# A hybrid decoder step on one core: the decode reads its cache tiles at a fixed place in the product stream, and the FFN norm's column sums move behind the first index's products

## The chip, the core and the metric

The kernel runs on one core of a Trainium2 chip. The time is the device time of one execution, in microseconds (us). The core has a matrix engine (PE, with its weight loads as PEld), a vector engine (DVE), a scalar engine (ACT), a general engine (POOL) and a queue engine (SP). Each works through its own list of instructions in order; semaphores tie them together, and DMA queues move data beside them. POOL issues the gathers of the decode cache, SP nearly all other loads.

## What is computed

One layer of a decoder, for a prompt of 512 tokens and for eight decode samples with a past of 2048 tokens each, in float32:

```python
a = rms_norm(x, attn_norm); proj = a @ w_in
# 8 stick-breaking attention heads (prompt: causal; sample: over the paged cache)
z = q.k * SCALE + bias;  log_1m_beta = log_sigmoid(z) - z
att = exp(log_sigmoid(z) + reverse_cumsum(log_1m_beta) - log_1m_beta);  o_sb = rms_norm(att @ v)
# 8 gated DeltaNet heads: conv width 4, silu, l2 norm, decay g, chunked recurrence on a state
s = s * exp(g) + k (beta * (v - k.s));  o_gdn = rms_norm(q.s) * silu(z_gate)
h = x + concat(o_sb, o_gdn) @ w_out
f = rms_norm(h, ffn_norm)
h = h + (silu(causal_dwconv(f @ w_gate)) * (f @ w_up)) @ w_down
h = h + (p @ w_ple_proj) * sigmoid(rms_norm(h, ple_norm) @ w_ple_gate);  y = rms_norm(h, final_norm)
```

For the samples, `k` and `v` of the attention are 2 x 64 MB of cache rows picked by a page table, and the DeltaNet state `s` is 4 MB.

## The kernel before

All 520 tokens (512 and 8) stand as two halves of 260 columns. A product is sixteen steps of the contraction in three float32r splits (high by high, high by low, low by high) in two halves: 96 matmuls, with the weights cut in `weights` (L234) into a high part (`wh`, ACT, L242) and a low part (`wl`, DVE, L243), one pair for each half-product of eight steps. The text counts places in the mixing stage by these half-products.

**Stages.** Up to about 85 us norm and a small projection; then 56 products with `w_in`; between them, on queues called lanes, the chains of each head (`sb_chain`, `k_chain`, `gdn_chain`, `invert`). A chain is a generator that yields the time after which it wants to go on; `tick` (L205) moves a clock by 0.65 for each step of a product and runs the chains that are due. Their small matmuls go through `mmq` and `trq` (L222, L226), which pin them behind the product matmul issued last. Then `w_out` in two parts: part 0 takes twelve of the sixteen heads (16 products of 72 matmuls), part 1 the last four heads (16 of 48). The half-products are counted from 1; `w_out` starts with number 113. From 1214 us on the FFN runs: 43 indices of `strassen` (seven block products each, names `pa` to `pd`), then `w_down`, the gate of the per-layer input and the last norm.

**Decode.** The cache comes as 128 tiles `kv` of 1 MB (32 of K for four heads, 32 of V, and the same for the other four), in two buffers. `gather` (L405) issues four indirect DMAs for each on POOL. Each K tile is used by four DVE instructions `dacc` (L435), each V tile by four `junk` (L465); after the last K tile stand a softplus, a scan and a small matmul `pc`. The DeltaNet state is read in four tiles (`rec`), with `gtmp` (L1013) and reduces (L1015) on DVE, in `delta_decode` (L965); its result `mix_s[2]` goes into the columns of the samples of heads 8 to 15, ahead of part 0 of `w_out`.

These calls stand in the program at a few points. What they issue has a priority far behind (`later(30000)`), so that the scheduler, which places each instruction by simulated time, puts them wherever an engine would else be idle:

```python
    with tc.issue_after(last.ins):
        decode_v(0, 0, AFTER)
    decode_v(0, AFTER)
```

Here the first two V tiles of the first four heads are pinned behind the last instruction of a triangular solve (`X`, L679 to L681). `AFTER` and `VSPLIT` are both 2: `decode_v(1, 0, 2)` stands ahead of `delta_decode()`, `decode_v(1, 2)` behind it.

**FFN norm.** While `w_out` part 1 ends, each row block `h` is squared on ACT (`sqt`) and summed by accumulating DMAs into two tiles `acc` (L1166). `rstd_of` (L278) sums these over partitions with matmuls (`ssq`, L286) and builds the scale `rb` (L288). It is called behind the first `strassen`, with matmuls that nothing pins.

## Time and profile before

| | us |
|---|---|
| median of 3 runs (lowest, highest) | 2807.46 (2803.03, 2808.61) |
| the profiled execution, its own time | 2818.48 |
| its span, first to last instruction | 2816.7 |
| PE busy | 2665.9 |
| DVE busy | 1900.4 |
| ACT busy | 1158.0 |
| POOL busy | 707.0 |

The rows below come from the profiled execution. A start is counted in us from the start of its span. `[3.60 <-DMA kv]` means: the engine stood idle for 3.60 us before this instruction, and a DMA into `kv` ended that. A busy PE is not PE at its peak; the granted clock (PEclk) says how fast it was allowed to run, 1.00 for 2.4 GHz, 0.50 for 1.2 GHz.

### The profile page before, as it was taken

The numbers are of one execution on the slowest core, as the hardware profiler recorded it, in microseconds if no ns is written. First come the engines' busy times: TensorE is split into PE (matmuls) and PEld (weight loads), VectorE is DVE, ScalarE is ACT, GpSimd is POOL, SyncE is SP. The second block draws the span as 40 slices with busy tenths as digits, with TensorE's granted clock in tenths as the row PEclk, the third lists the DMA queues.
The fourth block names the chain that finished last, engine by engine and source line by source line (L and its number), as shares of the span: only waits on it lengthen the run. The fifth ranks groups of instructions, "written<-read, shape, count | busy, mean of one in ns | idle before, by whom it ended". The sixth has DMA issues, their size and how long they took to land.

```text
span 2816.7 us, 52568 instructions
## 1 busy us (share of the span) xinstructions
PE 2665.9 (95%) x21329; PEld 2601.5 (92%) x21329; DVE 1900.4 (67%) x3060; ACT 1158.0 (41%) x1936; POOL 707.0 (25%) x773
## 2 busy tenths in 40 slices
PE   8998899899899988979999999999999999999997
PEld 7898788898898878979999999999998999999997
DVE  7477766667779776678888888888885242433545
ACT  5454434333345542554444444444452121322433
POOL 4565646556650556210000000000000000000000
PEclk9999999999999999989999999999999999999998
DMA  5778777767775778676555656565657453433333
GB/s 187 229 248 263 226 209 240 230 218 238 245 239 151 245 239 257 178 220 177 164 175 162 183 160 177 161 179 163 177 158 243 133 155 92 136 98 93 111 114 114
DMA packets 194083, 519.99 MB, mean 185 GB/s; under 512 B 41712, under 2 KB 51824, under 8 KB 193328
## 3 DMA queue, kind: packets, MB, share of 16 engines
q1 hardware_dynamic: 138672, 336.13, 37.3%
q0 software_dynamic: 55168, 180.50, 22.1%
q8 instruction: 167, 2.74, 0.4%
q14 instruction: 76, 0.62, 0.1%
HBM read 463.05 MB, written 49.76 MB: 182 GB/s over the span
## 4 chain that ended last, share of the span: by engine, by line
PE 59%; DVE 12%; DMA 11%; issue 9%; POOL 4%; ACT 3%; SPq 1%; another core or an unknown queue 0%; DVEq 0%; POOLq 0%; ACTq 0%
PE mm L264 27%; PE pb L1197 13%; PE pc L1197 9%; PE pa L1197 4%; POOL kv L408 4%; PE pd L1197 4%; DMA kv<-in_ck,idx 3%; DMA kv<-in_cv,idx 3%; DVE dacc L435 2%; DVE wl L243 2%; DMA acc<-sqt 2%; DVE junk L465 1%; DVE yg L610 1%; DVE dpart L1015 1%; DMA out_recs<-st 1%
## 5 line engine op out<-in xcount | busy, mean ns | idle before, releaser
L264 PE MATMUL mm<-ah,wl 128*128 128x260 f32 x4128 | 858.5, 289 | 27.3 <-DVE wl L243 21.9
L264 PE MATMUL mm<-ah,wh 128*128 128x260 f32 x4128 | 862.0, 290 | 14.1 <-ACT wh L242 11.0
L264 PE MATMUL mm<-al,wh 128*128 128x260 f32 x4128 | 855.3, 288 | 4.4 <-DVE al L373 3.1
L264 PEld LDWEIGHTS mm<-ah,wl 128*128 128x128 f32 x4128 | 651.2, 192 | 38.4 <-DVE wl L243 26.8
L264 PEld LDWEIGHTS mm<-ah,wh 128*128 128x128 f32 x4128 | 652.5, 192 | 22.2 <-ACT wh L242 12.6
L264 PEld LDWEIGHTS mm<-al,wh 128*128 128x128 f32 x4128 | 650.8, 192 | 8.8 <-DVE al L373 3.9
L242 ACT CAST wh<-w 128x1024 fp32r<-128x1024 f32 (+4 forms) x289 | 279.6, 968 | 670.9 <-PE mm L264 588.9
L243 DVE TENSOR_TENSOR wl<-w,wh 128x1024 fp32r<-128x1024 f32 (+4 forms) x282 | 315.7, 1120 | 232.2 <-ACT wh L242 218.9
L408 POOL DMA_INDIRECT kv<-in_cv,idx x256 | 282.2, 1102 | 275.7 <-DVE junk L465 86.5
L408 POOL DMA_INDIRECT kv<-in_ck,idx x256 | 287.3, 1122 | 188.2 <-DVE dacc L435 89.3
L1192 ACT CAST wh<-a 128x1024 fp32r<-128x1024 f32 x172 | 181.0, 1052 | 368.0 <-PE pc L1197 193.0
L465 DVE SCALAR_TENSOR_TENSOR junk<-kv,dacc 128x512 f32<-128x512 f32 x256 | 176.4, 689 | 104.2 <-DMA kv<-in_cv,idx 82.2
L1193 DVE TENSOR_TENSOR wl<-a,wh 128x1024 fp32r<-128x1024 f32 x172 | 210.0, 1221 | 46.2 <-ACT wh L1192 46.0
L435 DVE SCALAR_TENSOR_TENSOR dacc<-kv,qd,dacc 128x512 f32<-128x512 f32 x252 | 178.3, 746 | 90.9 <-DMA kv<-in_ck,idx 69.4
L1197 PE MATMUL pb<-ah,wl 128*128 128x260 f32 x774 | 221.5, 286 | 1.5 <-DVE wl L1193 1.3
L1197 PE MATMUL pb<-ah,wh 128*128 128x260 f32 x774 | 219.8, 284 | 0.6 <-ACT wh L1192 0.6
L1197 PE MATMUL pb<-al,wh 128*128 128x260 f32 x774 | 219.3, 283 | 0.0
L1356 POOL TENSOR_TENSOR y<-h,fr 128x260 f32<-128x260 f32 x8 | 6.9, 887 | 682.2 <-DVE fr L1351 682.2
L1197 PEld LDWEIGHTS pb<-ah,wl 128*128 128x128 f32 x774 | 147.0, 190 | 3.5 <-DVE wl L1193 2.7
L597 POOL MEMSET cbf<- 128x2 f32 x43 | 4.3, 99 | 573.4 <-DVE yf L610 566.4
L1197 PEld LDWEIGHTS pb<-ah,wh 128*128 128x128 f32 x774 | 146.5, 189 | 1.4 <-ACT wh L1192 1.4
L1197 PEld LDWEIGHTS pb<-al,wh 128*128 128x128 f32 x774 | 146.8, 190 | 0.0
(435 smaller groups left out, 4741.1 us busy)
## 6 DMA issues: line engine op xcount, KB each, us to landing
w<-in_w_in SPq DMA_DIRECT2D x112, 512.0 KB
a<-in_w_up SPq DMA_DIRECT2D x86, 512.0 KB
w<-in_w_down SPq DMA_DIRECT2D x48, 512.0 KB
w<-in_w_gate SPq DMA_DIRECT2D x43, 512.0 KB
s<-in_w_up SPq DMA_DIRECT2D x43, 512.0 KB
a<-in_w_gate SPq DMA_DIRECT2D x43, 512.0 KB
s<-in_w_up POOLq DMA_DIRECT2D x43, 512.0 KB
w<-in_w_pg SPq DMA_DIRECT2D x32, 512.0 KB
```

The lines of the kernel that those rows point to most:

```text
L242: S.copy(wh, w)
L243: last_wl[0] = (eng or V).tensor_tensor(wl, w, wh.bitcast(F32), op=ALU.subtract).ins
L264: last_mm[0] = PE.matmul(ps[:, hf, 0:HALF], lhsT=a, rhs=b[:, hf * HALF:(hf + 1) * HALF], start=(first and n == 0), stop=(last and n == 2)).ins
L408: G.indirect_dma_start(out=t[:, pg], out_offset=None, in_=src, in_offset=bass.IndirectOffsetOnAxis(ap=idx[:, g, dc, pg:pg + 1], axis=0))
L435: V.scalar_tensor_tensor(a2[dd % 2], kt[:, :, d], qd[:, dd:dd + 1], a2[dd % 2], op0=ALU.mult, op1=ALU.add)
L465: V.scalar_tensor_tensor(junk, vt[:, :, d], 1.0, A, op0=ALU.mult, op1=ALU.mult, accum_out=ov[:, dc * DC + d:dc * DC + d + 1])
L610: V.scalar_tensor_tensor(y, cb[:, j:j + L], cw[:, j:j + 1], y, op0=ALU.mult, op1=ALU.add)
L1015: V.tensor_reduce(part, tmp.rearrange("p k v -> p v k"), axis=AX.X, op=ALU.add)
L1192: S.copy(wh, w)
L1193: V.tensor_tensor(wl, w, wh.bitcast(F32), op=ALU.subtract)
L1197: last_mm[0] = PE.matmul(ps, lhsT=a[:, k], rhs=b, start=(start and k + n == 0), stop=(k == NP - 1 and n == 2), skip_group_check=not start).ins
L1356: e.tensor_tensor(y[:, j], hres[m + j][:, c], r, op=ALU.mult)
```

## The change

One generator, `decode()`, on a lane of its own called `kv`, takes the place of the three kinds of calls. It takes the tiles in one order: K and V of heads 0 to 3, K of heads 4 to 7, eleven V tiles (`DELTA`), the four state tiles of the DeltaNet, and the other 21 V tiles. It asks to be resumed every 4.1 of the clock (`PACE`). Each time it places the instructions of one tile behind the last `wl` issued (`paced`), with a priority of 60 instead of 30000, and then issues the loads of the next tile but one into the buffer it frees. There are still two buffers; the state tiles now pass through them as tiles like the others. The decode's small matmuls go through `mmq` and `trq`. The pin on the solve's last instruction stays only as the value that `last_dve` holds from there to the next `wl`.

Ahead of part 0 of `w_out` the program runs the lane until the DeltaNet's result is there, and ahead of part 1 until it is done. The memset of the 24 tiles `cbg` goes from POOL to DVE. `rstd_of` behind the first index takes `mmq`. Three small stores of the state's decode go into `delta_decode`, and in `w_down` the load of these and the start of the state's update move from index 1 to indices 2 and 4.

```diff
-LATE = 30000
-VSPLIT = 2
-AFTER = 2
+PACE = 4.1
+DELTA = 11
...
+        if eng is None:
+            last_dve[0] = last_wl[0]
...
-    def rstd_of(parts, rp):
+    def rstd_of(parts, rp, mm=None):
+        mm = mm or PE.matmul
...
-                PE.matmul(ps[:, 0:HALF], lhsT=ones, rhs=a[:, c], start=(n == 0), stop=(n == len(parts) - 1))
+                mm(ps[:, 0:HALF], ones, a[:, c], start=(n == 0), stop=(n == len(parts) - 1))
...
+    kv_items = [(n, g, dc) for g in range(2) for n in ("ck", "cv") for dc in range(NDC)]
+    at = 3 * NDC + DELTA
+    kv_items[at:at] = [("rec", 0, c) for c in range(4)]
...
+    def kv_fetch():
+        if not kv_items:
+            return
+        n, g, dc = kv_items.pop()
         t = dpool.tile([P, 4, DC * PAGE], F32, name="kv", bufs=2)
+        kv_ring.append((n, g, dc, t))
+        if n == "rec":
+            nc.sync.dma_start(t.rearrange("p a c -> p (a c)"), i["rec"][:, dc * 2048:dc * 2048 + 2048])
+            return
         for pg in range(4):
-            G.indirect_dma_start(out=t[:, pg], out_offset=None, in_=src,
+            G.indirect_dma_start(out=t[:, pg], out_offset=None, in_=i[n],
...
+    def paced():
+        st = contextlib.ExitStack()
+        if last_dve[0] is not None:
+            st.enter_context(tc.issue_after(last_dve[0]))
+        st.enter_context(later(60))
+        return st
...
+    def pace():
+        kv_time[0] += PACE
+        return max(0.0, kv_time[0] - clock[0])
...
+            for dc in range(NDC):
+                if g and dc == DELTA:
+                    while not cs_ready:
+                        yield 1.0
+                    yield from delta_decode()
+                yield pace()
+                vt = kv_take("cv", g, dc).rearrange("p g (d t) -> p g d t", d=DC)
+                with paced():
+                    for d in range(DC):
+                        junk = n4(dpool.tile([P, 8 * PAGE], F32, name="junk")[:, :4 * PAGE])
+                        V.scalar_tensor_tensor(junk, vt[:, :, d], 1.0, A, op0=ALU.mult, op1=ALU.mult,
+                                               accum_out=ov[:, dc * DC + d:dc * DC + d + 1])
+                kv_fetch()
...
-        G.memset(cb[:, 0:hw], 0.0)
+        (G if rs is not None else V).memset(cb[:, 0:hw], 0.0)
...
-    with tc.issue_after(last.ins):
-        decode_v(0, 0, AFTER)
-    decode_v(0, AFTER)
+    last_dve[0] = last.ins
...
         if part:
-            drain("sb")
+            drain("sb", "kv")
+        else:
+            until("kv", ("dec", 2))
...
-            rstd[0] = rstd_of(accs, npool)
+            rstd[0] = rstd_of(accs, npool, mmq)
...
-                    if m == 1:
+                    if m == 2:
...
-                if m == 1:
+                if m == 4:
                     spawn("upd", delta_update(*kvg, gpool))
```

What the built programs hold at three places follows, first of before, then of after. On DVE, where the solve of `X` ends and the first V tile is used (`tb` and `X` are the solve's):

```order
L681 TENSOR_TENSOR X<-X,tb 128x3x29
L679 TENSOR_TENSOR tb<-blk,X 128x60
L681 TENSOR_TENSOR X<-X,tb 128x2x30
L679 TENSOR_TENSOR tb<-blk,X 128x31
L681 TENSOR_TENSOR X<-X,tb 128x31
L465 SCALAR_TENSOR_TENSOR junk,ov<-kv,dacc_1199 128x512
L685 COPY XT<-X 128x1024
L465 SCALAR_TENSOR_TENSOR junk,ov<-kv,dacc_1199 128x512
```

```order
L722 TENSOR_TENSOR tb<-blk,X 128x112
L724 TENSOR_TENSOR X<-X,tb 128x4x28
L506 SCALAR_TENSOR_TENSOR junk,ov<-kv,dacc_1332 128x512
L722 TENSOR_TENSOR tb<-blk,X 128x87
L812 SCALAR_TENSOR_TENSOR osb<-osb,vec,sqh 128x512
L506 SCALAR_TENSOR_TENSOR junk,ov<-kv,dacc_1332 128x512
L724 TENSOR_TENSOR X<-X,tb 128x3x29
L842 SCALAR_TENSOR_TENSOR z<-pz,mb 128x128
L506 SCALAR_TENSOR_TENSOR junk,ov<-kv,dacc_1332 128x512
```

The first tile's four `junk` and two of the next now stand between the last steps of the solve, and no longer behind them.

On PE, the DeltaNet decode's two last small matmuls (`po<-cst,of`, then `pn`), which `mix_s[2]` waits for; `po<-z,vtok` belongs to an attention chain, `ah_11085` is head 8, the first of `w_out` part 0 whose sample columns come from `mix_s[2]`:

```order
L264 MATMUL mm<-al_504,wh 128x260 x2
L264 MATMUL mm<-ah_503,wl 128x260 x2
L264 MATMUL mm<-ah_505,wh 128x260
L1031 MATMUL po<-cst,of 128x64
L264 MATMUL mm<-ah_505,wh 128x260
L264 MATMUL mm<-al_506,wh 128x260 x2
```

```order
L222 MATMUL pi<-sm,ones 128x384
L222 MATMUL po<-z,vtok 128x512
L222 MATMUL po<-z,vtok 128x384
L222 MATMUL po<-z,vtok 128x256
L222 MATMUL po<-z,vtok 128x128
L222 MATMUL po<-cst,of 128x64
L222 MATMUL pn_9941<-sq_9891,ones 128x64
L265 MATMUL mm<-ah_11085,wh 128x260 x2
L265 MATMUL mm<-al_11086,wh 128x260 x2
```

Before, the first of them lay inside a product of `w_in`; now both lie inside the first half-product of `w_out`, right ahead of the matmul that needs the result, and behind the chain's.

On PE, where the FFN begins (`ssq` are the norm's column sums, `pb` and `pa` block products of the first index, `pc` its third):

```order
L264 MATMUL mm<-ah_12728,wh 128x260 x2
L264 MATMUL mm<-al_12729,wh 128x260 x2
L264 MATMUL mm<-ah_12728,wl 128x260 x2
L286 MATMUL ssq<-acc_13371,ones 128x260 x2
L286 MATMUL ssq<-acc_13372,ones 128x260 x2
L1197 MATMUL pb<-ah_13331,wh 128x260
L1197 MATMUL pb<-al_13332,wh 128x260
```

```order
L1237 MATMUL pc<-ah_13369,wh 128x260
L1237 MATMUL pc<-al_13370,wh 128x260
L1237 MATMUL pc<-ah_13369,wl 128x260
L222 MATMUL ssq<-acc_13371,ones 128x260 x2
L222 MATMUL ssq<-acc_13372,ones 128x260 x2
L1237 MATMUL pb<-al_13338,wh 128x260
```

The eight passes of `ssq` moved from ahead of the first block product to 190 rows behind it, past all the block products of the first index and into those of the second.

## Rows read from the trace of the kernel before

**Rows 1.** The page: engine, busy us (share of the span), instructions.

```profile
PE 2665.9 (95%) x21329; PEld 2601.5 (92%) x21329; DVE 1900.4 (67%) x3060; ACT 1158.0 (41%) x1936; POOL 707.0 (25%) x773
```

**Rows 2.** Busy time by stretch: from:to, length, engines, granted clock, DMA share, GB/s.

```profile
833.00:914.00 81.00, 77.78 (x609) 73.48 (x607) 74.32 (x136) 46.67 (x88) 5.08 (x4) 1.00 0.57 174
914.00:1140.00 226.00, 201.86 (x1442) 185.76 (x1443) 160.62 (x368) 90.51 (x136) 130.33 (x120) 0.95 0.75 244
1140.00:1214.00 74.00, 73.78 (x606) 72.72 (x604) 51.72 (x96) 48.62 (x89) 18.39 (x27) 1.00 0.69 188
1214.00:1242.00 28.00, 13.29 (x59) 11.14 (x60) 17.57 (x30) 12.69 (x23) 4.74 (x7) 0.63 0.83 237
```

**Rows 3.** What PE waited for, 60 to 1130 us: us, times, longest.

```profile
PE mm L264 <- DVE wl L243: 15.2, 12, 3.4
PE po L224 <- ACT z L835: 8.3, 3, 3.9
```

**Rows 4.** The cache tile kv: duration min/median/max in ns, first to last start.

```profile
L408 POOL DMA_INDIRECT kv<-in_cv,idx x256: 940/947/2782, 331.9 to 1133.0; - x128
L435 DVE SCALAR_TENSOR_TENSOR dacc<-kv,qd,dacc x252: 724/746/809, 104.5 to 832.4; 128x512 f32<-128x512 f32 x126
L465 DVE SCALAR_TENSOR_TENSOR junk<-kv,dacc x256: 673/691/749, 358.5 to 1140.0; 128x512 f32<-128x512 f32 x128
```

**Rows 5.** POOL in order of time: start, us, instruction, idle before and its releaser.

```profile
1055.17 0.95 POOL L408 DMA_INDIRECT kv<-in_cv,idx  x1 [0.31 <-issue]
1058.92 0.95 POOL L408 DMA_INDIRECT kv<-in_cv,idx  x1 [0.30 <-issue]
1068.43 0.94 POOL L408 DMA_INDIRECT kv<-in_cv,idx  x1 [0.80 <-DVE junk L465]
```

**Rows 6.** DVE in order of time, the same tiles.

```profile
1057.65 0.75 DVE L465 SCALAR_TENSOR_TENSOR junk<-kv,dacc 128x512 f32<-128x512 f32 x1 [3.60 <-DMA kv<-in_cv,idx]
1064.52 0.68 DVE L465 SCALAR_TENSOR_TENSOR junk<-kv,dacc 128x512 f32<-128x512 f32 x1
1067.46 0.69 DVE L465 SCALAR_TENSOR_TENSOR junk<-kv,dacc 128x512 f32<-128x512 f32 x1
```

**Rows 7.** DVE groups by line: busy, mean ns, idle before and releasers.

```profile
L465 DVE SCALAR_TENSOR_TENSOR junk<-kv,dacc 128x512 f32<-128x512 f32 x256 | 176.4, 689 | 104.2 <-DMA kv<-in_cv,idx 82.2 <-issue 18.3 <-ACT dacc L451 0.2
L435 DVE SCALAR_TENSOR_TENSOR dacc<-kv,qd,dacc 128x512 f32<-128x512 f32 x252 | 178.3, 746 | 90.9 <-DMA kv<-in_ck,idx 69.4 <-issue 21.5
L1015 DVE TENSOR_REDUCE dpart<-gtmp 128x64 f32<-128x1024 f32 x14 | 27.7, 1979 | 0.0
L1013 DVE TENSOR_TENSOR gtmp<-st,qkv 128x1024 f32<-128x1024 f32 x16 | 19.5, 1217 | 0.0
```

**Rows 8.** POOL groups by line.

```profile
L408 POOL DMA_INDIRECT kv<-in_cv,idx x256 | 282.2, 1102 | 275.7 <-DVE junk L465 86.5 <-DVE seed L866 75.5 <-issue 61.8
L597 POOL MEMSET cbg<- 128x3 f32 x24 | 2.6, 112 | 10.7 <-DVE yg L610 10.1 <-issue 0.5
```

**Rows 9.** DVE: last use of first K, first of second V, first wl of w_out.

```profile
340.23 0.75 DVE L435 SCALAR_TENSOR_TENSOR dacc<-kv,qd,dacc 128x512 f32<-128x512 f32 x1
846.76 0.69 DVE L465 SCALAR_TENSOR_TENSOR junk<-kv,dacc 128x512 f32<-128x512 f32 x1 [0.19 <-ACT dacc L451]
982.63 0.95 DVE L243 TENSOR_TENSOR wl<-w,wh 128x768 fp32r<-128x768 f32 x1
```

**Rows 10.** PE, DVE and ACT where the FFN begins.

```profile
1225.95 2.10 PE L286 MATMUL ssq<-acc,ones 128*128 128x260 f32 x4 [12.16 <-DMA acc<-sqt]
1232.77 0.58 PE L1197 MATMUL pb<-ah,wh 128*128 128x260 f32 x1 [0.64 <-ACT wh L1192]
1225.29 1.23 DVE L1219 TENSOR_TENSOR a<-a,a 128x1024 f32<-128x1024 f32 x1 [2.31 <-DMA a<-in_w_up]
1231.30 0.48 ACT L288 ACTIVATE rb<-ssq,eps 128x260 f32<-128x260 f32 x1 [7.75 <-PE ssq L286]
1231.68 1.04 ACT L1192 CAST wh<-a 128x1024 fp32r<-128x1024 f32 x1
```

More of the change, by code (lines that the diff above doesn't have):

```diff
@@ L48 @@
 IH = 1
-EARLY = 3000
 PPT = 12
@@ L421, in decode_k @@
                           qs[g].rearrange("d h b -> d b h").unsqueeze(3).broadcast_to([P, B, 4, 4]))
+            yield I_L
             pq = pstd("pq")
-            PE.transpose(pq[:, :P], qr, C("ident"))
+            trq(pq[:, :P], qr)
             qd = dpool.tile([P, P], F32, name="qd")
             S.copy(qd, pq[:, :P])
-        a2 = [dpool.tile([P, 4, PAGE], F32, name=f"dacc{j}") for j in range(2)]
-        for dc in range(NDC):
-            with later(LATE):
-                kt = gather(i["ck"], g, dc)
-                for d in range(DC):
-                    dd = dc * DC + d
-                    if dd < 2:
-                        V.tensor_scalar(a2[dd], kt[:, :, d], qd[:, dd:dd + 1], None, op0=ALU.mult)
-                    else:
-                        V.scalar_tensor_tensor(a2[dd % 2], kt[:, :, d], qd[:, dd:dd + 1], a2[dd % 2],
-                                               op0=ALU.mult, op1=ALU.add)
@@ new lines, in decode @@
+            a2 = [dpool.tile([P, 4, PAGE], F32, name=f"dacc{j}") for j in range(2)]
+            for dc in range(NDC):
+                yield pace()
+                kt = kv_take("ck", g, dc).rearrange("p g (d t) -> p g d t", d=DC)
+                with paced():
+                    for d in range(DC):
+                        dd = dc * DC + d
+                        if dd < 2:
+                            V.tensor_scalar(a2[dd], kt[:, :, d], qd[:, dd:dd + 1], None, op0=ALU.mult)
+                        else:
+                            V.scalar_tensor_tensor(a2[dd % 2], kt[:, :, d], qd[:, dd:dd + 1], a2[dd % 2],
+                                                   op0=ALU.mult, op1=ALU.add)
+                kv_fetch()
@@ new lines, in decode @@
+            s, t1 = [x.rearrange("p a b -> p (a b)") for x in a2]
+            V.tensor_tensor(s, s, t1, op=ALU.add)
+            S.activation(s, s, AF.Identity, bias=VC("sbbd", g), scale=SCALE)
+            S.activation(t1, s, AF.Abs)
+            S.activation(t1, t1, AF.Exp, scale=-1.0)
+            S.activation(t1, t1, AF.Ln, bias=1.0)
+            V.scalar_tensor_tensor(t1, s, 0.0, t1, op0=ALU.max, op1=ALU.add)
+            inc = dpool.tile([P, 8 * PAGE], F32, name="inc", tag="junk")[:, :T]
@@ new lines, in decode @@
+            yield S_N
+            po = pstd("po")
+            mmq(po[:, :32], ov, C("seld"))
+            of = dpool.tile([P, 32], F32, name="os")
+            S.copy(of, po[:, :32])
+            sq = dpool.tile([P, 32], F32, name="sqs")
+            S.activation(sq, of, AF.Square)
+            yield S_N
+            pn = pstd("pn")
+            mmq(pn[:, :32], C("ones"), sq)
+            S.activation(sq, pn[:, :32], AF.Ln, bias=eps, scale=1.0 / HD)
+            S.activation(sq, sq, AF.Exp, scale=-0.5)
@@ L551, in program @@
     V.tensor_scalar(neg, eg[:, 0], -1.0, None, op0=ALU.mult)
-    decode_k(0)
+    spawn("kv", decode())
     close()
@@ L989, in delta_decode @@
         for a, nm in enumerate(("ra", "rb")):
-            PE.matmul(pab2[:, 8 * a:8 * a + 8], lhsT=C(nm)[:32], rhs=abs_, start=True, stop=True)
+            mmq(pab2[:, 8 * a:8 * a + 8], C(nm)[:32], abs_)
         for a in range(2):
@@ L997, in delta_decode @@
         S.activation(egd, gd, AF.Exp)
-        def state(c):
-            t = dpool.tile([P, 2, 1024], F32, name="st", tag="kv", bufs=2)
-            nc.sync.dma_start(t.rearrange("p a c -> p (a c)"), i["rec"][:, c * 2048:c * 2048 + 2048])
-            return t
         sqk = dpool.tile([P, 2, 64], F32, name="sqk")
-        with later(LATE):
-            for c in range(4):
-                t = state(c)
-                for a in range(2):
-                    ch = c * 2 + a
-                    s3 = t[:, a].rearrange("p (k v) -> p k v", v=64)
+        for c in range(4):
+            t = kv_take("rec", 0, c).rearrange("p (a e) c -> p a (e c)", a=2)
+            for a in range(2):
+                yield pace()
+                ch = c * 2 + a
+                s3 = t[:, a].rearrange("p (k v) -> p k v", v=64)
+                with paced():
                     for w, vecp in enumerate((qp, kp)):
@@ L1070, in program @@
     nc.sync.dma_start(o["vs"], vs)
-    kvgd = [dp.tile([P, w], F32, name=f"kvgd{w}") for w in (P, 64, 1)]
-    for t, x in zip(kvgd, dd):
-        nc.sync.dma_start(t, x)
     for part in range(2):
```

103 lines of the change are left out of this document (48 added, 55 removed).

## The prediction

> **What bounds the kernel now.** The page says that PE is busy for 2665.9 of 2816.7 us [rows 1], so at most some 150 us can be had, and the question is where PE is not full. The view of busy time by stretch answers it. From 1140 to 1214 us, where no cache tile is read any more, PE is busy for 73.78 of 74.00 us; from 914 to 1140, with V tiles in flight, for 201.86 of 226, and the granted clock falls to 0.95 there; across the border to the FFN, 1214 to 1242, for 13.29 of 28 at a clock of 0.63 [rows 2]. The time to win lies in the mixing stage and at that border.
>
> Next, who ends last in the mixing stage. The waits of PE before a product's matmul name DVE's `wl` [rows 3]. DVE is not short of time: its own groups show that it idles 90.9 us before `dacc` and 104.2 before `junk`, mostly for the DMA of a cache tile [rows 7]. So the chain is: a tile is not there, DVE stands at it, the `wl` behind it comes late, PE stands. In the timeline the loop closes: POOL issues a V tile from 1055.17 on, in four steps of 1.25 us (the last at 1058.92); DVE uses it first at 1064.52 and last at 1067.46; at 1068.43, released by that last use, POOL begins the tile two further on [rows 5, 6]. Two tiles share two buffers, so a tile takes (1068.43 - 1055.17) / 2 = 6.63 us, and neither engine is busy for all of it: 4.7 us of the loop are landing, some 3.7 use. 128 tiles at that pace are 849 us. They take from 104.5 to 1140.6, that is 1036 us [rows 4]. 75.5 of the difference is one pause of POOL while the state tiles sit in the buffers [rows 8]; the other 112 us are phase changes, waits of POOL, and tiles used later than they landed.
>
> **The change, part by part.** All terms are against the profiled execution, 2818.5 us.
>
> *Order up to the second V cache (until 833 us).* The built orders place nearly every tile behind the same `wl` as before: of 98 tiles the first use stands at most two half-products away. The four uses of a tile also span the same instructions. Two buffers stay, and a load is still issued when a buffer comes free. So "even" changes little in the order, and the 6.63 us stay. What can be won is the part of the 112 us that comes from tiles used later than they landed, less the phase changes (14 us each: last `dacc` 832.4, first `junk` 846.76 [rows 4, 9]). I take 10 us off, with ends of +5 and -50; it is the softest term.
>
> *First V tile ahead of the solve's end.* V gathers began at 331.9, so the first tile had landed by some 342 (331.9, four steps of 1.25 and 4.7 of landing), yet its first use is at 358.5 [rows 4]. In the new order it stands in the solve, six of the solve's steps earlier. The softplus chain needs 14 us at the other phase change; the last `dacc` of the first one began at 340.23 [rows 9], which leaves 358.5 - (341 + 14), about 4 us, and the third tile's gather can start that much earlier again. I take -6, ends -10 and 0.
>
> *Memsets.* 24 of 0.112 us leave POOL; POOL idled 10.7 us ahead of them, held by DVE's `yg` [rows 8], with gathers queued behind. Only what delays a late tile counts: -5, ends -13.3 and 0. On DVE they cost 2.7 us, in gaps.
>
> *From 833 us to the end of `w_out`.* Before, the state decode ran first (833 to 914, PE 77.78 of 81, DVE 74.32 [rows 2]) with POOL paused; then thirty V tiles bound the stream until 1140, and 74 us of pure products remained. A half-product of `w_out` part 0 is short: 606 matmuls in 73.78 us are 0.122 each [rows 2], so 4.4 us for its 36. Now eleven tiles come first over ten half-products: the phase change, 8 us for the two that wait, nine times 6.63, so until about 915; PE needs 75 for them (833 to 982.63 for twenty [rows 9]), so until 908: +7. The state's 16 `gtmp` and 16 reduces cost 16 x (1.217 + 1.979) = 51 us of DVE as before [rows 7] and stand beside the last ten half-products of `w_in`, where before eight V tiles stood: +3. Three V tiles, whose loads came long before, then stand in one heap with the end of the state decode, right at the first half-product of `w_out`. There PE has 24 matmuls (2.9 us) and then needs `mix_s[2]`: an attention chain's eleven small matmuls, two round trips PE to ACT and back, and on DVE a dozen cache instructions of 0.77 stand before it. PE's waits of this sort were up to 3.9 us each [rows 3]; here four follow each other: 12 us, ends 5 and 20. Against that, only 18 tiles are left from there instead of 21, 20 us of stream less, while three more half-products (13 us) remain behind the last: that can free at most what PE could not use before, 226 - 202 = 24 us; I take 12. Sum +7 + 3 + 12 - 12 = +10, ends -5 and +25.
>
> *FFN border.* The first `ssq` came at 1225.95, 12.16 us late, for the accumulating DMA; the next four later still; ACT's `rb` waited in front of the first weight cast (1231.31, then 1231.68), and the first block product began at 1232.77 [rows 10]. Moved behind the index, `ssq` and `rb` hold nothing. What is late next is the loads of the first index: DVE's sum of two weight tiles began at 1225.29, waiting for `a` [rows 10]. So the start can come up to 7.5 us earlier, but the second block needs that sum and a further one. -4, ends -8 and 0. The eight passes then cost some 2 us of PE wherever they stand.
>
> *Moves in `w_down`, the three stores.* The load and the update lie in `w_down`, under a PE that is busy for 95% of the span [rows 1]; the three small stores now pass SP ahead of the loads of `w_out`, whose weights lie two ahead: 0, and if that cover is gone some 2 us for three issues on SP.
>
> Sum: -10 - 6 - 5 + 10 - 4 = **-15 us**, 2803.5 against 2818.5. The profiled execution is 0.4% above the median; on the median's scale this is 2807.46 x 2803.5 / 2818.5 = **2792.5 us**.
>
> The Trainium skill, "Perfetto Trace Analysis", section Optimization Strategy, says that the same gap repeating on the engine that should be full can mean that buffers are too few. It speaks against this change, which keeps two buffers; the repeated gap of DVE (3.60 us before 1057.65 [rows 6]) agrees with it, and rival 3 is what it would give.
>
> The Trainium skill, "DMA: Bandwidth & Descriptors", section Anatomy of one DMA, gives 2.0 us plus the bytes over 436e3 for a DMA issued by POOL, 2.6 for a gather of 256 KB. The trace shows 4.7 from last issue to first use here; with the page's figure a tile would take 5.6 us, an estimate, and the mixing stage would have room that it does not show.
>
> **Rivals.**
>
> *1. Even use sets the stream free (faster by more).* If most of the 112 us, less two or three phase changes of 14, is loss by tiles used late, then a consumer that never falls behind takes 50 off instead of 10: -55, so 2764 on the profile and 2752 on the median's scale. For it: 86.5 us of POOL's idle time ahead of the V gathers ended with a `junk` [rows 8]. Against: the order places the uses where they were. Chance 0.18.
>
> *2. The heap at the border and longer tiles (slower).* Counted with the durations of the trace, the four uses of one of the last 32 tiles span 5.1 us in the new order, 4.05 before. Half of that is added to each tile's 6.63: 29 tiles by 0.5 are 15 us. With the heap at its end of 20 instead of 12 (+8) and no gain from evenness (+10) the sum is -15 + 33 = +18, 2825 on the median's scale. The point that decides is the stretch from 833 on: above +25 it eats all the other gains. For it: DVE is at 74.32 of 81 us during the state decode, with no room for tiles. Chance 0.27.
>
> *3. The stream as it was.* The order changes nothing, the loop of 6.63 stays, the gain at the border to the FFN and of the memsets pays for the heap: -10 + 10 to -5, 2803 to 2807. This is also what it would be if the change did not do what it says. Chance 0.15.
>
> **How the numbers follow.** The forecast, 2783 to 2803, has 0.40. A measurement of this kernel tells 0.2%, 5.6 us, from no change; so faster means below 2801.8. Faster: rival 1 and 0.35 of the forecast, 0.53. Same: 0.05 and rival 3, 0.20. Slower: rival 2, 0.27. The range takes in the forecast, rival 3, most of rival 2 (2815 to 2835) and the weak end of rival 1 (2740 to 2775): 2765 to 2829.
>
> **What would show it.** By stretch, the end of the last product of `w_out` should come at some 1203 us instead of 1214; the last `junk` near 1125; the first V tile used near 354. The gap of POOL of 75.5 us before a gather should be gone, the loop of two tiles still be 13 us. PE should show one heap of waits near 990 to 1010, of 5 to 20 us, on ACT and DVE. The first block product of the FFN should follow the last of `w_out` by 12 to 17 us, not 19, with no `ssq` between. If the loop of two tiles is shorter than 13 us, the model of the stream is wrong; if the heap is above 25 us, rival 2; if `dacc` and `junk` idle as before and the stage ends where it ended, rival 3.

## The result and the profile after

The changed kernel takes 2835.86 us (median of 7; 2823.76 to 2841.73) beside 2807.46 of the kernel before (7 runs). The ratio is **1.0084, interval 1.0065 to 1.0103: slower by some 24 us**. The forecast was 2792.5 with a range up to 2829: the kernel became slower instead of faster, and the time lies above the range. Run beside each other twice more, the ratio was 1.0077 (1.0053 to 1.0102) and 1.0096 (1.0072 to 1.0120).

The page of the profiled execution of after (2828.47 us; span 2826.6), busy us by engine, and PE by slices of the span. They answer to [rows 1]; PE is busy for 9 us less in a span 10 us longer.

```profile
span 2826.6 us, 52561 instructions
...
PE 2656.5 (94%) x21329; PEld 2593.5 (92%) x21329; DVE 1904.3 (67%) x3084; ACT 1159.4 (41%) x1936; POOL 711.1 (25%) x749
...
PE   8998899899899888989999999999998999999997
```

Two profiled executions that differ by 10 us do not show 24: the first profile of before ran at 2818.48, above its own median. So three profiles of after and two of before were laid side by side. The `wl` instructions, 590 in each kernel and the same weights in the same rank, serve as milestones; a stage is the time from the start of the `wl` of one rank to that of another (rank counted from 0). In us:

| stage (ranks of `wl`) | before, two profiles | after, three | DELTA = 6, two | DELTA = 16 | half tiles |
|---|---|---|---|---|---|
| first K cache (12 to 44) | 257.0, 258.8 | 256.0, 257.7, 254.4 | 257.5, 253.5 | 257.7 | 235.5 |
| first V cache (44 to 72) | 263.3, 256.8 | 257.4, 254.4, 256.2 | 255.5, 255.7 | 260.6 | 259.9 |
| second K cache (72 to 100) | 228.9, 227.0 | 226.4, 230.0, 232.6 | 232.2, 230.3 | 227.6 | 231.1 |
| rest of `w_in` (100 to 116) | 139.3, 137.3 | 144.9, 143.3, 144.5 | 137.9, 140.0 | 141.2 | 133.2 |
| **border to `w_out`** (116 to 120) | 27.7, 27.9 | **48.4, 47.6, 47.7** | 29.9, 29.5 | **72.5** | 30.0 |
| `w_out` part 0 (120 to 144) | 139.3, 139.6 | 130.0, 129.4, 131.3 | 136.9, 139.7 | 126.5 | 120.2 |
| `w_out` part 1 (144 to 164) | 69.2, 69.1 | 67.6, 66.9, 67.8 | 68.9, 67.8 | 68.8 | 66.6 |
| border to the FFN (164 to 180) | 65.6, 66.6 | 65.5, 64.0, 67.1 | 65.3, 66.0 | 65.9 | 64.5 |
| FFN (180 to 460) | 806.4, 807.2 | 807.4, 810.9, 808.7 | 809.9, 808.8 | 808.4 | 807.4 |
| start of `w_down` (460 to 490) | 159.5, 160.1 | 164.0, 169.4, 163.4 | 163.8, 161.9 | 166.4 | 161.4 |

By the means of after less before: up to the second K cache -4 us in all, the rest of `w_in` +6, the border to `w_out` **+20**, `w_out` -11, the FFN's border and the FFN +2, the start of `w_down` +6. With the first 85 us (-1) that is +18, and the spans of these five profiles differ by 17.6 (2830.8 against 2813.2 in the mean). The medians differ by 24 to 28, so 6 to 10 us of the loss have no place in these profiles. The table also answers the forecast by stretch: the last product of `w_out` ends at 1218.2 in the first profile of after, 1213.8 in that of before, where 1203 was expected.

**The heap at the border.** PE of after in order of time, where `w_out` begins (start, us, instruction, idle before and its releaser):

```profile
980.24 0.40 PE L265 MATMUL mm<-al,wh 128*128 128x260 f32 x2
980.47 0.40 PE L265 MATMUL mm<-ah,wl 128*128 128x260 f32 x2
981.49 0.92 PE L222 MATMUL pi<-l,cst 128*128 128x128 f32 x4 [0.62 <-DVE l L850]
...
986.14 1.65 PE L222 MATMUL pi<-l,cst 128*128 128x384 f32 x2 [3.50 <-DVE z L875]
...
993.56 3.63 PE L222 MATMUL po<-z,vtok 128*128 128x512 f32 x8 [2.08 <-ACT z L876]
996.99 0.52 PE L222 MATMUL po<-cst,of 128*128 128x64 f32 x2
998.82 0.43 PE L222 MATMUL pn<-sq,ones 128*128 128x64 f32 x2 [1.30 <-ACT sq L1075]
1003.78 0.80 PE L265 MATMUL mm<-ah,wh 128*128 128x260 f32 x2 [4.53 <-ACT ah L185]
```

and DVE of after there, the end of the state decode:

```profile
989.15 1.88 DVE L1053 TENSOR_REDUCE dpart<-gtmp 128x64 f32<-128x1024 f32 x1
...
992.25 0.69 DVE L506 SCALAR_TENSOR_TENSOR junk<-kv,dacc 128x512 f32<-128x512 f32 x1
...
995.19 0.08 DVE L506 DVE_READ_ACCUMULATOR junk<-kv,dacc 128x1 f32 x1
...
998.04 0.69 DVE L506 SCALAR_TENSOR_TENSOR junk<-kv,dacc 128x512 f32<-128x512 f32 x1
...
1001.99 0.28 DVE L1081 SCALAR_TENSOR_TENSOR og<-og,vec,sq 128x64 f32<-128x64 f32 x1 [3.26 <-ACT sq L1080]
1002.31 0.27 DVE L1082 TENSOR_TENSOR mix_s<-og,zs 128x64 f32<-128x64 f32 x1
1003.76 0.70 DVE L186 TENSOR_TENSOR al<-mx,ah 128x520 fp32r<-128x520 f32 x1 [1.18 <-ACT ah L185]
```

After 24 matmuls PE is out of products at 980.87 and begins the next at 1003.78. In between stand only the attention chain's and the state decode's small matmuls, each behind a DVE or ACT step. Of the 12.0 us that PE is idle there, 6.2 come before steps of the attention chain (0.62, 3.50 and 2.08) and 5.8 behind the state decode's `po` (1.30 before `pn`, 4.53 before head 8). On DVE these are the last reduce of the state at 989.15, the eight `junk` of the heap from 992.25 to 998.73 with `of` among them, then PE, ACT, PE, ACT, `og` at 1001.99, `mix_s` at 1002.31, the cast and `al` of head 8. Busy time by stretch (from:to, length, PE, PEld, DVE, ACT, POOL, granted clock, DMA share, GB/s), of after and then of before:

```profile
980.00:1006.00 26.00, 13.96 (x43) 8.86 (x42) 19.90 (x44) 11.02 (x25) 11.98 (x12) 0.72 0.50 145
```

```profile
982.00:1006.00 24.00, 19.81 (x133) 18.36 (x132) 19.11 (x43) 12.40 (x17) 11.94 (x12) 0.86 0.77 264
```

DVE is busy for 19.90 of 26 us and PE has 43 instructions against 133. The two matmuls at 1003.78 take 0.80 us where those at 980.47 took 0.40: the granted clock (0.72 in this stretch, a mix of its two levels) is still low just behind the pause.

Not all of the +20 is lost. In before, the attention chain's eight `po` that now stand in the gap lay among the products of `w_out` part 0:

```profile
1007.86 2.32 PE L224 MATMUL po<-z,vtok 128*128 128x512 f32 x8
```

So some twenty small matmuls moved from the later stage into the earlier one. PE's time in the two stages, in us, as means of two profiles of before and three of after:

| | products | small matmuls (number) | idle |
|---|---|---|---|
| border, before | 20.0 | 4.1 (18) | 3.8 |
| border, after | 21.2 | 14.4 (40) | 12.4 |
| `w_out` part 0, before | 110.3 | 15.1 (51) | 14.2 |
| `w_out` part 0, after | 108.7 | 7.6 (32) | 14.0 |

The two stages together cost 11 us more: 8.4 of idle time, and 2.8 for small matmuls that run at the lower clock or came from `w_in`. Of the 9 us that part 0 is shorter, 7.5 are the matmuls that left it; its idle time stayed.

### The profile page after: what moved, and what is told of

Same layout as the page of the kernel before. It is cut to its first block, busy times and chain, and to the rows that moved or that the text cites. A ratio compares the mean times of both kernels' runs of the same rounds, so it can differ in the third digit from the quotient of the medians.

```text
span 2826.6 us, 52561 instructions
## 1 busy us (share of the span) xinstructions
PE 2656.5 (94%) x21329; PEld 2593.5 (92%) x21329; DVE 1904.3 (67%) x3084; ACT 1159.4 (41%) x1936; POOL 711.1 (25%) x749
## 4 chain that ended last, share of the span: by engine, by line
PE 54%; DMA 16%; issue 10%; DVE 9%; POOL 8%; ACT 2%; SPq 0%; POOLq 0%; DVEq 0%; ACTq 0%
PE mm L265 23%; PE pb L1237 13%; PE pc L1237 8%; POOL kv L424 8%; DMA kv<-in_ck,idx 6%; DMA kv<-in_cv,idx 5%; PE pa L1237 4%; PE pd L1237 4%; DVE dacc L476 1%; DMA acc<-sqt 1%; DVE junk L506 1%; DVE wl L242 1%; DMA out_recs<-st 1%; DVE dpart L1053 1%; DMA st<-in_rec 1%
## 5 line engine op out<-in xcount | busy, mean ns | idle before, releaser
L265 PEld LDWEIGHTS mm<-ah,wl 128*128 128x128 f32 x4128 | 650.5, 192 | 52.3 <-DVE wl L242 48.7
L242 DVE TENSOR_TENSOR wl<-w,wh 128x1024 fp32r<-128x1024 f32 (+4 forms) x282 | 315.7, 1120 | 236.1 <-ACT wh L241 231.1
L424 POOL DMA_INDIRECT kv<-in_ck,idx x256 | 294.4, 1150 | 197.3 <-DVE dacc L476 71.4
```

The source lines that it names most:

```text
L242: last_wl[0] = (eng or V).tensor_tensor(wl, w, wh.bitcast(F32), op=ALU.subtract).ins
L265: last_mm[0] = PE.matmul(ps[:, hf, 0:HALF], lhsT=a, rhs=b[:, hf * HALF:(hf + 1) * HALF], start=(first and n == 0), stop=(last and n == 2)).ins
L424: G.indirect_dma_start(out=t[:, pg], out_offset=None, in_=i[n], in_offset=bass.IndirectOffsetOnAxis(ap=idx[:, g, dc, pg:pg + 1], axis=0))
```

## The experiments

Five sessions on four chips. In two of them (the runs e1 to e4, and e8 to e11) the kernel before itself took 2830 us instead of 2807 to 2816; the same chip gave both values, and no run tells why. Ratios are therefore always against before in the same session, and the comparison of two sessions is left to the stages above. The changed kernel itself was never run in a session where before took 2830; its ratio of 1.008 to 1.010 holds for the others.

**Is it the heap? More of it, and none of it.** DELTA is the number of V tiles ahead of the state decode. With 16, ten of its sixteen pieces stand at the first half-product of `w_out`; with 2 or 6, the decode ends ahead of it. DELTA = 16 is run e7:

```diff
-DELTA = 11
+DELTA = 16
```

> The changed kernel with DELTA = 16: sixteen V tiles ahead of the state tiles, so that nearly the whole state decode (ten of its sixteen pieces) stands at the first half-product of w_out instead of its end alone. Theory A (PE waits there for the state decode's result): ten pieces of 3.2 us more, some 30 us on top of the changed kernel's loss there, ratio 1.009 to 1.016 against before. Theory B (waits for wl all along): as the changed kernel, within 5 us.

Measured: 2855.11, ratio **1.0152** (1.0122 to 1.0182). The border takes 72.5 us instead of 48; against the changed kernel of the same session (2836.27) the time grows by 19 us, not by 30. PE of this kernel there:

```profile
991.45 3.66 PE L222 MATMUL po<-z,vtok 128*128 128x512 f32 x8 [3.17 <-ACT z L876]
1023.46 0.69 PE L222 MATMUL po<-cst,of 128*128 128x64 f32 x2 [28.35 <-DVE of L1068]
...
1030.22 0.80 PE L265 MATMUL mm<-ah,wh 128*128 128x260 f32 x2 [4.79 <-ACT ah L185]
```

PE waits 28.35 us in one piece for DVE's `of`, the last step of the state decode ahead of `po`. That is theory A. DELTA = 2 is run e4:

```diff
-DELTA = 11
+DELTA = 2
```

> The changed kernel with DELTA = 2 instead of 11: the state tiles come behind two V tiles, as they did before, and no tile stands in a heap at the border to w_out. Theory A (the heap, PE without 24 matmuls' cover waiting for the state decode's end): the stage's loss goes and the 8 to 11 us that the trace shows ahead of the border stay, so about 2795 to 2812, ratio 0.996 to 1.002. Theory B (uses pinned behind each wl make DVE stand for tiles with the next wl behind them, all through the stage; PE's waits on wl doubled from 15 to 34 us): it stays at 1.005 to 1.010, with PE's waits on wl above 25 us.

Measured: 2822.83 beside 2830.53 of before, 0.9977 (0.9961 to 0.9994); the border takes 29.9 us. The ratio is in theory A's range; the time is not, since before took 2830 here. PE's waits on `wl` did not fall below 25 us (25.8), but they say little about the change: in a second profile of before (f1, below) they are nearly as long as in after. Waits of PE for a product's weights, 60 to 1130 us, of f1 and of after:

```profile
PE mm L264 <- DVE wl L243: 29.2, 22, 3.6
```

```profile
PE mm L265 <- DVE wl L242: 33.9, 23, 5.1
```

The six profiles with the decode as before have 15 to 29 us of these waits, the ten with the new order and whole tiles 19 to 34. So theory B fell: 15 against 34 us, on which it stood, was for the most part a difference between two executions.

**The parts alone.** The decode, the memset and the three stores alone (e3, repeated as e9) are the changed kernel with these two edits taken back:

```diff
-            rstd[0] = rstd_of(accs, npool, mmq)
+            rstd[0] = rstd_of(accs, npool)
...
-                    if m == 2:
+                    if m == 1:
...
-                if m == 4:
+                if m == 1:
```

> The changed kernel with the ssq edit and the w_down edit undone: the decode's sequence and the memset alone. If the heap at the first half-product of w_out carries the loss, this has all but some 5 us of it: ratio 1.004 to 1.008 against before. If the w_down edit carried more than the profile shows, it falls to 1.000 to 1.003. In the trace the wl of equal rank should be some 10 us ahead of before up to the border and some 5 to 15 behind it after.

> The decode's sequence and the memset alone (DELTA = 11, ssq and w_down as before), repeated for the same reason. The changed kernel stands at 1.0077 here, the w_down edit should take 0.002 of it and ssq 0 to -0.001: 1.005 to 1.007. Rival: 1.001 as in the first session.

Measured: 1.0014 (0.9996 to 1.0031) and 1.0011 (0.9991 to 1.0030), both in the sessions where before took 2830; as times, 2834.64 and 2832.35, 1 to 6 us below the changed kernel's 2836 to 2839 of other sessions. Its two profiles hold 48.7 and 48.6 at the border and 160.9 and 161.2 at the start of `w_down`. The expected ratio did not come; in the second run the rival's 1.001 did. By stage the heap is there in full, but ahead of the border these kernels do not lead before by 10 us: the `wl` of rank 116 starts at 977 us in both, at 974 and 965 in the two profiles of before.

The `ssq` edit alone, on the kernel before (e1, repeated as e10):

```diff
-            rstd[0] = rstd_of(accs, npool)
+            rstd[0] = rstd_of(accs, npool, mmq)
```

> The kernel before with one edit: the FFN norm's ssq matmuls go through mmq. From the profile of the changed kernel, where the first block product began 14.5 us after the border's last w_out matmul as against 19 before but waited again at 1238.96 and 1240.21, the theory that each part has its own price says 0 to -3 us (ratio 0.999 to 1.000), first block product some 10 us after the last product of w_out, and later waits that give it back. The prediction's term was -4 us. The rival, that the norm's late scale delays the first index's conv and what uses it, says +5 us or more.

> The ssq edit alone, repeated. In the first session 0.9984 (0.9965 to 1.0003). Theory: -2 to -4 us, 0.9985 to 0.9995, the border to the FFN shorter by that. Rival: nothing (1.000), since the first index's later products wait for their casts instead.

Measured: 0.9984 (0.9965 to 1.0003) and 1.0005 (0.9986 to 1.0024): nothing that can be told. The profile of after shows where the gain goes (PE, ACT, DVE and POOL, in order of time):

```profile
1217.83 0.40 PE L265 MATMUL mm<-ah,wl 128*128 128x260 f32 x2
1228.34 0.58 PE L1237 MATMUL pb<-ah,wh 128*128 128x260 f32 x1 [10.11 <-ACT wh L1232]
...
1238.96 0.39 PE L1237 MATMUL pc<-ah,wh 128*128 128x260 f32 x1 [1.98 <-ACT wh L1232]
1237.86 1.04 ACT L1232 CAST wh<-s 128x1024 fp32r<-128x1024 f32 x1 [8.10 <-DMA s<-in_w_up]
1237.85 1.22 DVE L1260 TENSOR_TENSOR a<-s,a 128x1024 f32<-128x1024 f32 x1 [4.91 <-DMA s<-in_w_up]
1227.11 1.21 POOL L1244 DMA_DIRECT2D s<-in_w_up  x1
1232.58 0.88 POOL L1244 DMA_DIRECT2D s<-in_w_up  x1 [4.26 <-DMA s<-in_w_up]
```

The first block product begins 10.1 us after the last product of `w_out`, where before has 19.0 (the 14.5 of the expectation mixes the two traces); in the profiles of e1 and e10 it is 9.7 and 9.5. Then PE waits again, here at 1238.96, for the cast of the sum `s` of two weight tiles, which arrives by two accumulating loads on POOL's queue at 1237.85. From 1240 to 1250 the granted clock is 0.66, so low for two thirds of the time, against 1.00 in before. By stretch, before and after:

```profile
1240.00:1250.00 10.00, 9.68 (x81) 9.48 (x80) 5.20 (x6) 4.89 (x8) 0.84 (x1) 1.00 0.53 172
```

```profile
1240.00:1250.00 10.00, 9.15 (x51) 8.86 (x52) 5.30 (x6) 3.10 (x6) 0.87 (x1) 0.66 0.52 170
```

The `w_down` edit alone, on the kernel before (e2, repeated as e8):

```diff
-                    if m == 1:
+                    if m == 2:
...
-                if m == 1:
+                if m == 4:
```

> The kernel before with one edit: in w_down the small loads move from index 1 to 2 and the start of the state's update from 1 to 4. In the two profiles the wl of equal rank stand 5.2 us apart at the last FFN index and 10 to 12 us after the first w_down products. If this edit causes it: +5 us (ratio 1.002), with PE waits on wl between the fourth and the eighth product of w_down. If the difference there came from the runs and not from the edit: 0 (0.999 to 1.001).

> The w_down edit alone on the kernel before, repeated, since the session of the first four runs showed the kernel before itself 18 us slower than in the other sessions. The five profiles with this edit lose 5 to 10 us (mean 7) from the last FFN index to the end against the first profile of before, the four without it 0 to 4 (mean 1.5). Theory: the update's traffic lies later, so that w_down's start is disturbed twice: +4 to +7 us, ratio 1.0015 to 1.0025. Rival (from the runs): 0.999 to 1.001.

Measured: 1.0004 (0.9983 to 1.0024) and 0.9991 (0.9974 to 1.0009). By time the edit cannot be told from nothing. By stage it can, with a small overlap: the start of `w_down` takes 163.4 to 169.4 us in the seven profiles with the edit (mean 166.2) and 158.9 to 163.8 in the eleven without (mean 161.3). The state's update by tile, first and last start, of before and of a profile of after (after_again):

```profile
L1054 DVE SCALAR_TENSOR_TENSOR st<-st,kvg,up x16: 745/751/754, 2118.6 to 2184.9; 128x512 f32<-128x512 f32 x16
```

```profile
L1097 DVE SCALAR_TENSOR_TENSOR st<-st,kvg,up x16: 744/751/753, 2143.6 to 2205.4; 128x512 f32<-128x512 f32 x16
```

It ends 20.5 us later; 7.6 of these stand already at the start of `w_down`. Counted from the `wl` of rank 460, its last instruction starts at 102 to 106 us in six profiles without the edit and at 111 to 116 in the seven with it, and PE, which in before was full again from 2190 on, loses 4 us there. By stretch, of before and after_again:

```profile
2190.00:2210.00 20.00, 20.00 (x169) 20.00 (x169) 5.23 (x6) 4.00 (x4) 0.00 (x0) 1.00 0.45 141
```

```profile
2190.00:2210.00 20.00, 15.67 (x108) 15.26 (x107) 9.11 (x12) 2.47 (x3) 0.00 (x0) 0.83 0.71 226
```

Five us would be a ratio of 1.0018. The first interval holds that, the second ends at 1.0009. So a cost of 5 us is what the stages show and the times do not confirm; what gives it back elsewhere, if anything does, stays open.

DELTA = 2 with the `w_down` edit taken back (e5):

> The changed kernel with DELTA = 2 and the w_down edit undone. The profiles of e2, e4 and the changed kernel lose 5 to 10 us at the start of w_down. If the edit does that: 5 us below DELTA = 2 alone, ratio 0.994 to 0.997, and the wl of equal rank stand no further behind before after the first w_down products than at the last FFN index (e3, without the edit: +2). If it came from the runs: 0.996 to 0.999 as with DELTA = 2 alone.

Measured: 2816.11 beside 2812.04, 1.0016 (0.9997 to 1.0035). That is outside both ranges, which start from a ratio of a session where before took 2830. As a time it is 6.7 us below DELTA = 2 alone (2822.83), across two sessions, and the start of `w_down` takes 158.9, as the edit's price asks; against before it is no gain. DELTA = 6, also without that edit (e11):

> The changed kernel with DELTA = 6 and the w_down edit undone: the state decode ends some four half-products before w_out begins, no heap, and four V tiles more than with DELTA = 2 are done by then. With DELTA = 2 and the edit undone the kernel stood at 1.0016. If POOL's pause and the tail after w_in still bind: 0.998 to 1.001. If the gathers ahead of the state decode only move waits: 1.000 to 1.003.

Measured: 0.9965 (0.9947 to 0.9983), 2821.26 us, below both ranges, in a session where before took 2830.

**Is it the changed kernel or the session?** The changed kernel once more in the second session, and then before (f1), after (f2) and DELTA = 6 (f3) in one session:

> The changed kernel once more, unedited, beside its parts on the same chip. The parts so far stood at 1.0014 (decode and memset), 0.9984 (ssq) and 1.0004 (w_down) of before. If the parts add: 1.000 to 1.004. If the first comparison (1.0084) holds on every chip: 1.006 to 1.010, and then something that only all edits together have costs another 15 us.

Measured: 2836.27 beside 2812.04, 1.0077 (1.0053 to 1.0102). The parts (1.0014, 0.9984, 1.0004) do not add up to it; they were measured where before took 2830.

> The kernel before, unedited, as a run of its own, so that its profile stands beside those of its session. In two sessions it took 2812 and 2807, in two others 2830. Theory A (only the kernel before, with its order of fillers, takes longer in those sessions): 2805 to 2833 as its session has it, and in a slow one its cache tiles between 340 and 870 us take 10 to 15 us more than in the first profile. Theory B (everything takes longer there): the loss spreads over the FFN and w_down too. Ratio 1.000 in any case.

> The changed kernel, unedited, a third time. It took 2836 in both sessions in which it ran. Theory A: 2832 to 2838 again whatever the kernel before does, so a ratio of 1.002 in a session where before takes 2830 and of 1.008 where it takes 2812. Theory B: 1.0065 to 1.010 in both, 2836 or 2854.

> DELTA = 6 with the w_down edit undone, a second time. It took 2821 where before took 2830. By Theory A 2815 to 2824 in any session, 12 to 18 below the changed kernel (heap 10 to 13, w_down 5). By Theory B 0.9965 of before in any session.

Measured: 1.0004 (0.9986 to 1.0023), **1.0096** (1.0072 to 1.0120) and 1.0023 (1.0005 to 1.0041); 2814.83, 2838.73 and 2818.42 us. The changed kernel has 2836 to 2839 in its three sessions. DELTA = 6 has 2821 where before took 2830 and 2818 where it took 2813: that speaks for theory A, that only the kernel before takes longer in some sessions. (The changed kernel came just above theory A's 2838.) Side by side, taking the heap and the `w_down` edit away gives 20 of the 25 us back. What is left of DELTA = 6 against before, 0.2%, is not traced to a step. What lifts the kernel before in two sessions stays open: none of them held a profile of before itself, and the four profiles of its near copies there (e1, e2, e8, e10) differ from it in no stage by the same amount. Together they point at the mixing stage: from rank 12 to rank 164 they take 1125 to 1144 us, where the two profiles of before take 1125 and 1117, and in the FFN 806 to 810, where those take 806 and 807.

**What sets the pace at all.** The changed kernel with only the first two tiles loaded (e6):

```diff
+        if len(kv_kept) == 2:
+            kv_ring.append((n, g, dc, kv_kept[len(kv_items) % 2]))
+            return
```

> The changed kernel with only the first two cache tiles loaded; every later use, the state's too, reads one of these two. This leaves out 126 tiles' gathers and the four state loads, so the decode's values are others. All DVE, ACT and PE instructions stay. If the loop of two buffers sets the mixing stage's end: the stage loses most of what it stands above PE's own work, 80 to 130 us, so 2700 to 2745, and the heap at the border still shows, 10 to 20 us. If DVE's load or the chains set it: under 40 us less.

Measured: 2693.73, 0.957 (0.9543 to 0.9597), 143 us below the changed kernel, more than expected. The heap, expected to stay with 10 to 20 us, is not there, and the border takes 24.3 us: the state's pieces stand seven half-products earlier, behind the `wl` of ranks 103 to 111 instead of 110 to 118. So this run takes the heap away as well as the loads. DVE's groups of this kernel (the same instructions as before, idle time last):

```profile
L482 DVE SCALAR_TENSOR_TENSOR dacc<-kv,qd,dacc 128x512 f32<-128x512 f32 x252 | 178.9, 743 | 0.2 <-DVE tb L728 0.2
L512 DVE SCALAR_TENSOR_TENSOR junk<-kv,dacc 128x512 f32<-128x512 f32 x256 | 175.7, 686 | 4.7 <-ACT dacc L500 1.4
```

Hardly any idle time is left ahead of them, where before has 90.9 and 104.2 [rows 7]. This takes away issue, landing and traffic together. The last run (g1) leaves the loads and changes the loop: each tile in two halves of two pages, four buffers of half the size, on top of DELTA = 6 without the `w_down` edit:

```diff
-        t = dpool.tile([P, 4, DC * PAGE], F32, name="kv", bufs=2)
+        t = dpool.tile([P, 2, DC * PAGE], F32, name="kv", bufs=4)
...
-        for pg in range(4):
+        for pg in range(2):
```

(the lane is resumed twice as often; the uses `dacc`, `junk` and the state's run over one half each; a second column of sums is added at the end)

> f3 (DELTA = 6, w_down edit undone) with each cache tile cut in two halves of two pages, in four buffers of half the size: the same SBUF, the same gathers, twice as many uses of half the length (a half costs some 0.42 us instead of 0.72, so some 30 us more DVE work for K and as much for V). If the loop of two buffers sets the stage (gathers wait for a use that waits for the landing): a half's loop is 2.5 us of issue, 4 of landing and 2.4 of use, some 9 us over four buffers, so POOL's own 5 us for a tile becomes the bound instead of 6.6: 30 to 90 us less than f3, 2730 to 2790, and POOL idle before gathers halves. If the landing or HBM sets it: the pace per tile stays, within 10 us of f3, or slower by the added DVE work.

Measured: 2769.22 beside 2815.63 of the kernel before, **0.9834** (0.9800 to 0.9867): 46 us below before, and 49 below DELTA = 6 as it ran in another session (2818.42), in the range expected. The same gathers, the same bytes and more DVE work; DVE's groups of this kernel, and of DELTA = 6 (f3):

```profile
L477 DVE SCALAR_TENSOR_TENSOR dacc<-kv,qd,dacc 128x256 f32<-128x256 f32 x504 | 218.7, 480 | 64.2 <-DMA kv<-in_ck,idx 63.6
L508 DVE SCALAR_TENSOR_TENSOR junk<-kv,dacc 128x256 f32<-128x256 f32 x512 | 216.7, 423 | 24.6 <-DMA kv<-in_cv,idx 12.2 <-ACT dacc L495 2.0
```

```profile
L476 DVE SCALAR_TENSOR_TENSOR dacc<-kv,qd,dacc 128x512 f32<-128x512 f32 x252 | 178.8, 748 | 92.0 <-DMA kv<-in_ck,idx 92.0
L506 DVE SCALAR_TENSOR_TENSOR junk<-kv,dacc 128x512 f32<-128x512 f32 x256 | 176.7, 690 | 117.7 <-DMA kv<-in_cv,idx 113.2 <-ACT dacc L494 1.3
```

Busy time rises by 80 us (218.7 + 216.7 against 178.8 + 176.7), idle time falls from 209.7 to 88.8. The gain lies in the first K cache (235.5 against 255), `w_out` (186.8 against 207) and less in the rest of `w_in`. The first V cache and the second K cache gain nothing (259.9 against 255.6, 231.1 against 231.3); what sets their length no run shows. In `w_out` POOL's queue now runs nearly without pauses between the gathers:

```profile
986.05 0.95 POOL L424 DMA_INDIRECT kv<-in_cv,idx  x1 [0.30 <-issue]
987.30 1.12 POOL L424 DMA_INDIRECT kv<-in_cv,idx  x1 [0.30 <-DMA kv<-in_cv,idx]
988.72 0.94 POOL L424 DMA_INDIRECT kv<-in_cv,idx  x1 [0.30 <-DVE junk L508]
989.97 0.95 POOL L424 DMA_INDIRECT kv<-in_cv,idx  x1 [0.30 <-issue]
```

Over the whole cache POOL's idle time before gathers was expected to halve and did not: it falls from 465.9 to 403.1 us. POOL's groups of DELTA = 6 (f3) and of this kernel:

```profile
L424 POOL DMA_INDIRECT kv<-in_cv,idx x256 | 283.6, 1108 | 271.0 <-DVE gtmp L1051 80.6
L424 POOL DMA_INDIRECT kv<-in_ck,idx x256 | 294.7, 1151 | 194.9 <-DVE dacc L476 68.7
```

```profile
L424 POOL DMA_INDIRECT kv<-in_ck,idx x256 | 309.8, 1210 | 160.7 <-DVE dacc L477 63.7
L424 POOL DMA_INDIRECT kv<-in_cv,idx x256 | 281.3, 1099 | 242.4 <-DVE junk L508 95.0
```

Whether more buffers or shorter tiles give the gain is not separated.

## Why the prediction was wrong

- **What bounds the kernel** was read rightly in part. Without the loads the mixing stage (rank 12 to 164) is some 130 us shorter than in after (e6), and another ring shortens the first K cache and `w_out` (g1), so there the loop of two buffers sets the pace; for the first V cache and the second K cache it is not shown. The warning that the change leaves the loop as it is was right: from one tile's first gather to that of the tile two further on, the median in `w_out` part 0 is 13.2 and 13.7 us in the profiles of before, 13.4 to 13.5 in after, the 13 that the text names, and 11.4 in g1. The rule of the Trainium skill ("Perfetto Trace Analysis", Optimization Strategy) that repeated gaps can mean too few buffers agrees with g1: more and smaller buffers in the same space gave 1.7% against before.
- **Evenness, -10 (ends +5 and -50): the largest gain, and the term that had no row.** The order stood nearly as before, the text itself said that it changes little, and yet 10 us were taken off. Up to the second K cache the stages differ by -4 us in the mean, inside their scatter; memset (-5) and the earlier first V tile (-6) are in that sum as well. So of -21 up to there -4 came, and no run tests the memset alone. Rival 1 rested on the same hope and is gone.
- **The first V tile, -6:** the step from the last `dacc` to the first `junk` did shrink, from 17.5 us (both profiles of before) to 13.8 (all three of after), the 14 of the text. But the first K cache ended at 346.2 to 349.8 instead of 341.0 and 342.0, so the first V tile is used at 360.0 to 363.6, not near 354: no gain in time.
- **From 833 us on, +10 (ends -5 and +25): inside its ends at +15, with one term that did not come.** The rest of `w_in` came at +6 (the terms +7 and +3 make 10). The heap, priced at 12 with ends 5 and 20, was sized rightly: the stage that holds it took 20 more, but 9 of these are gone from `w_out` part 0, mostly small matmuls that changed places, and 11 remain. The step that failed here is the counter-term of -12, the hope that fewer tiles behind the heap let PE use what it could not use before: PE's idle time in part 0 is 14.0 us against 14.2, and part 1 is 2 us shorter. That the table's `w_out` stands at -11, near the -12, is a coincidence of where the stages are cut.
- **POOL's pause of 75.5 us** was expected to go. It is 65.62 in after, since the state tiles hold both buffers until DVE has used them, as they did in before:

```profile
900.24 1.28 POOL L424 DMA_INDIRECT kv<-in_cv,idx  x1 [0.30 <-DMA kv<-in_cv,idx]
967.14 0.94 POOL L424 DMA_INDIRECT kv<-in_cv,idx  x1 [65.62 <-DVE z L842]
```

- **FFN border, -4 (ends -8 and 0): the upper end was right.** The prediction named what is late next, the sum of two weight tiles, and still took half of the gain. The row of `a` with its DMA [rows 10] asked for 0. (The start 1231.31 in the text is 1231.30 in the row.)
- **`w_down`, 0: wrong by the stages,** which show 4 to 6 us; the times of the edit alone do not confirm it. The cover named was PE's busy share of the whole span; at the place itself, the first 160 us of `w_down`, PE is idle for 8 us in before and for 12 to 13 in after.
- **The ground of the sum.** 2818.48 us of the profiled execution was 0.4% above its median, which the text scaled away. The scatter of single executions (2798 to 2828 for before in one session) is twice the whole sum of -15.

In sum, the step that failed most is the gains: -25 us were taken (evenness, first V tile, memsets, FFN border) where the stages show about 5. Next comes the counter-term of -12, of which 2 came, then `w_down` and the FFN with 8 us that stood at nothing; the rest of `w_in` came 4 us cheaper. That makes -15 into the +18 of the profiles; the 6 to 10 us beyond, which the medians show, stay open. Rival 2, with a chance of 0.27, named the right direction at 2825, but only one of its three reasons came, that evenness gives little: the heap was no dearer than priced, and longer tiles did not come (the uses of one of the last 32 tiles span 3.7 us in after and 4.0 in before, where the text has 5.1 and 4.05).

## What to carry to other kernels

Count a gain only where a row names the wait that ends; "more even" is no such row. Where a chain's result is needed at the start of a new stage, look at how many matmuls stand ahead of the need: 24 of them cover 3 us, not a chain of 23. When one stage grows and the next one shrinks, split both into work and idle time before calling it a loss and a gain: here nearly half of the growth was work that had changed places. And where a ring of two buffers paces a stage, change the ring before the order: four halves in the same space were worth 46 us against before, and no order of the same ring was more than 0.4% faster than before.

## What the runs showed of the hardware

In after, PE's products of the FFN's first index ran at a granted clock of 0.66 from 1240 to 1250, a mix of the two levels, 2.4 and 1.2 GHz. PE had been back at work since 1228.34, with waits of 1.98, 0.75 and 0.64 us between 1238 and 1242. In before, where PE began at 1232.77 and waited for 0.32 us in that stretch, the clock was 1.00 from 1240 to 1250. So a shorter wait at the border (10.1 against 19.0 us) was followed by a longer time at the low clock, and the stage at the border to the FFN is 0.6 us shorter in the mean.

The time of one unchanged program, the kernel before, stood at 2812 in one session and 2830 in another on the same chip, with 17 and 35 runs. DELTA = 6 moved by 3 us between a session of each kind, and the changed kernel by 3 us among sessions of the first kind. No run explains it.
